# Gate products of three groups summed in two PSUM banks, and the order of the products and output tiles around them

## The chip, the cores and the metric

The kernel runs on one core of a Trainium2 chip. The metric is device time in microseconds (us); lower is better. The engines are named as the profile names them: PE (matmuls; PEld is its weight load), DVE (vector), ACT (scalar), POOL (general purpose), SP (which here only issues DMAs). PSUM is the memory that the PE writes: eight banks of 512 fp32 columns in each of 128 partitions.

## The reference

One layer of an encoder on 512 frames of width 1024. Three branches (gated linear attention, forgetting attention, attention into 256 memory tokens) are merged by sigmoid gates; an output projection and a squared-ReLU MLP follow. What the change touches is the merge:

```python
u = rmsnorm(h, g_mix[l])
proj = u @ w_in[l]                       # its last 3 x 1024 columns are the gates
y_gla = o_gla.reshape(B, S, GLA_V) @ w_gla_o[l]
y_mem = o_mem.reshape(B, S, MEM_W) @ w_mem_o[l]
gt = jax.nn.sigmoid(gates.reshape(B, S, N_BRANCH, D))
merged = gt[:, :, 0] * y_gla + gt[:, :, 1] * y_fox + gt[:, :, 2] * y_mem
h = h + merged @ w_out[l]
```

## The kernel before

Every fp32 operand is split into a high part (fp32r) and the remainder, and a matmul becomes three: high by high, high by low, low by high (`mm3`, lines 154 to 157). Weights come as raw tiles by DMA; `split_w` casts them on ACT to the high part (L145) and subtracts on DVE for the low part (L146).

The gates of the memory branch and of the gated-linear branch are computed in four groups, two for each branch (groups 0 to 3 here; `gate_group`, called at L1043 to L1050). A group makes four gate tiles of 128 channels by 512 frames, as two by two blocks, and does it by a Strassen-Winograd scheme: seven block products (numbered 1 to 7) in place of eight, on sums of weight blocks and sums of input blocks. The sums of inputs (S1 to S4, `lefts_1`, `lefts_2`) are made once, in group 0. The sums of weights are made by DMA: `plus` lets POOL issue a DMA that adds a block of weights in DRAM onto a tile in SBUF (L923). `total` and `other` are these two tiles; in turn `total` is the operand of products 1, 5, 6 and 4, and `other` of product 7. A sum can be issued only when the split that reads the tile before is done.

A product is 24 matmuls of 256 columns into one PSUM bank from a pool of four (`product`, L937), two halves `a` of 256 columns, each its own accumulation group. `take` (L946) then brings it out: the seven results are added in SBUF tiles `ct` by DVE (L932) after ACT copies of products 1 and 5 (L948, L953), and ACT takes tanh of the finished blocks (L935). Here c11, c12, c21 and c22 are the four blocks; c11 and c21 lie in one `ct` tile, c12 and c22 in the other.

Between the products stand the branch's own output tiles: `output(j)` is 12 matmuls of 512 columns into a bank of another pool of four (`a` in the profile); a group has four of them. `merge(j)` (L977) multiplies the gate into the output tile on DVE (L979), and POOL adds it to the accumulator `acc` (L980). In groups 2 and 3 ACT and DVE then split the accumulator for the output projection (L983, L984: `mh`, `ml`), which follows group 3 (L1089): it walks over four weight tiles and for each over four frame tiles, whose PSUM tiles come from the same pool as the output tiles.

The order on the PE is the order of the program. On the other engines a scheduler orders by its own model of time; `issue_after` adds constraints. Each engine runs its own list in order, so an instruction that waits holds up what is behind it. For groups 1 to 3 (`ready is None`) the order on the PE is: product 1, product 2, output j+2, product 5, output j+3, product 3, product 6, product 7, output j, product 4, output j+1. Group 0 starts while the stage before still runs and has an order of its own.

Of the kernel before, what the change touches and what calls it, by code (L numbers as in the profile page):

```python
# [13 lines left out]
AF = mybir.ActivationFunctionType  # L14
ALU = mybir.AluOpType
AX = mybir.AxisListType

P = 128
# [46 lines left out]
def hybrid_block(ctx, tc, chunks, wst, memT, xN, cols, gffn, gfin, wup, cst, out):  # L65
    nc = tc.nc
# [5 lines left out]
    def nm(s):  # L72
        uid[0] += 1
        return f"{s}_{uid[0]}"
# [10 lines left out]
    def mmt(shape=None):  # L85
        return pmm.tile(shape or [P, 512], F32, tag="mm", name=nm("mm"))

    def at_(shape=None):
        return pa.tile(shape or [P, 512], F32, tag="a", name=nm("a"))

    def f(ap):
        return ap.bitcast(F32)
# [27 lines left out]
    chunk_n, cast_now, low_now = [0], [None], [None]  # L120
# [21 lines left out]
    def split_w(raw):  # L142
        hi = wp.tile([P, 1024], F32R, tag="hi", name=nm("whi"))
        lo = wp.tile([P, 1024], F32R, tag="lo", name=nm("wlo"))
        cast = nc.scalar.copy(hi, raw)  # L145
        low_now[0] = nc.vector.tensor_tensor(lo, raw, f(hi), op=ALU.subtract).ins  # L146
        cast_now[0] = cast.ins
        next_sum(cast.ins)
        return hi, lo
# [4 lines left out]
    def mm3(ps, lh, ll, rh, rl, start, stop, on=False):  # L154
        nc.tensor.matmul(ps, lh, rh, start=start, stop=False, skip_group_check=on)  # L155
        nc.tensor.matmul(ps, lh, rl, start=False, stop=False, skip_group_check=on)  # L156
        nc.tensor.matmul(ps, ll, rh, start=False, stop=stop, skip_group_check=on)  # L157
# [29 lines left out]
    def run(*gens):  # L187
        for g in gens:
            for _ in g:
                pass  # L190
# [60 lines left out]
    with pool("front") as fp:  # L251
# [25 lines left out]
        ps = at_()  # L277
# [449 lines left out]
    with pool("gla") as lp:  # L727
# [115 lines left out]
        ready = []  # L843
# [4 lines left out]
        xsum = {}  # L848
# [13 lines left out]
    def h_tile(t, name):  # L862
        return hp.tile([P, D], F32, tag=f"h{t}", name=nm(name))
# [18 lines left out]
    with pool("outp") as op_:  # L882
        def own_tile(i, g):
            return op_.tile([P, 1024], F32R, tag=f"f{i}{g}", name=nm(f"f{i}{g}"))
# [4 lines left out]
        S1, S2, S4 = ([quad(own_tile(i, g)) for g in "hl"] for i in range(3))  # L889
# [9 lines left out]
                split(*S3, xsum[3])  # L899

        def lefts_2(to, block):
            with tc.issue_after(low_now[0]):
                nc.vector.tensor_tensor(xsum[1], block[0], xsum[1], op=ALU.subtract)
                nc.vector.tensor_tensor(xsum[1], xsum[1], block[1], op=ALU.add)
                cast = nc.scalar.copy(to[0], xsum[1]).ins
                nc.vector.tensor_tensor(to[1], xsum[1], f(to[0]), op=ALU.subtract)
            return cast
# [3 lines left out]
        def gate_group(gate, wo, oh, ol, i, ready=None, last=None):  # L911
            src = {b: wst[index["W", gate, i, b]] for b in ("11", "12", "21", "22")}
            total, other = (h_tile(2 * (i % 2) + n, "wb") for n in range(2))
            X = [op_.tile([P, 2, S], F32, tag=f"ct{n}", name=nm("ct")) for n in range(2)]
            (c11, c21), (c12, c22) = ([x[:, :, 256 * n:256 * n + 256] for n in range(2)] for x in X)
            nc.sync.dma_start(total, src["11"])
            first = nc.sync.dma_start(other, src["12"]).ins

            before = summed[0]

            def plus(to, b):
                with tc.issue_after(before) if before is not None else ExitStack():
                    summed[0] = nc.gpsimd.dma_start(to, src[b], accum_op=ALU.add).ins  # L923

            def block(b):
                raw = wp.tile([P, 1024], F32, tag="raw", name=nm("raw"))
                with tc.issue_after(first):
                    loaded[0] = nc.sync.dma_start(raw, src[b]).ins
                return raw

            def vec(to, x, y, op=ALU.add):
                nc.vector.tensor_tensor(to, x, y, op=op)  # L932

            def tanh(x):
                nc.scalar.activation(x, x, AF.Tanh, scale=0.5)  # L935

            def product(n, w):  # L937
                wh, wl = (t.rearrange("p (a k c) -> p a k c", a=2, k=4) for t in w)
                uh, ul = GATE[n]
                ps = mmt([P, 2, 256])  # L940
                for a in range(2):
                    for k in range(4):
                        mm3(ps[:, a, :], wh[:, a, k, :], wl[:, a, k, :], uh[:, k, :], ul[:, k, :], k == 0, k == 3)
                return ps

            def take(n, ps):  # L946
                if n == 1:
                    nc.scalar.copy(c21, ps)  # L948
                if n == 2:
                    vec(c11, c21, ps)  # L950
                    tanh(c11)
                if n == 5:
                    nc.scalar.copy(c22, ps)  # L953
                if n == 6:
                    vec(c21, c21, ps, ALU.subtract)
                    vec(c22, c22, c21, ALU.subtract)
                if n == 3:
                    vec(c12, c22, ps)
                    tanh(c12)
                if n == 7:  # L960
                    vec(c22, c22, ps, ALU.subtract)
                    tanh(c22)
                    vec(c21, c21, ps)
                if n == 4:
                    vec(c21, c21, ps)
                    tanh(c21)

            ys = {}

            def output(j):  # L970
                if j % 2 == 0:
                    with tc.issue_after(first):
                        ys["w"] = get_o(wo, j)
                ys[j] = at_()
                run(o_tile(ys["w"], j, oh, ol, ys[j]))

            def merge(j):  # L977
                th = X[j % 4 // 2][:, j % 2, :]
                nc.vector.scalar_tensor_tensor(th, th, 1.0, ys[j], op0=ALU.add, op1=ALU.mult)  # L979
                nc.gpsimd.tensor_tensor(acc[j], acc[j], th, op=ALU.add)  # L980
                if last is not None:
                    h, l = last
                    nc.scalar.mul(h[:, j, :], acc[j], 0.5)  # L983
                    nc.vector.scalar_tensor_tensor(l[:, j, :], acc[j], 0.5, f(h[:, j, :]), op0=ALU.mult, op1=ALU.subtract)  # L984

            j = 4 * i
            if ready is None:
                take(1, product(1, split_w(total)))
            if ready is not None:
                with tc.issue_after(first):  # L990
                    ys["w"] = get_o(wo, j + 2)
                p1 = product(1, ready[0])
                with tc.issue_after(low_now[0]), tc.issue_after(cast_now[0]):
                    lefts_1()
                    vec(total, total, other)
                    take(1, p1)
            else:
                plus(total, "12")
            plus(other, "22")
            take(2, product(2, ready[1] if ready else split_w(block("21"))))  # L1000
            if ready is None:
                output(j + 2)
            else:
                for n in (2, 3):
                    ys[j + n] = at_()
                    run(o_tile(ys["w"], j + n, oh, ol, ys[j + n]))
            w = split_w(total)
            cast = cast_now[0]
            p5 = product(5, w)
            plus(total, "22")  # L1010
            if ready is not None:
                cast = lefts_2(S2, A11)
                with tc.issue_after(cast):
                    take(5, p5)
                p7 = product(7, split_w(other))
            else:
                take(5, p5)
                output(j + 3)
                p3 = product(3, split_w(block("22")))
            with tc.issue_after(cast):  # L1020
                w = split_w(total)
            take(6, product(6, w))
            plus(total, "21")
            if ready is not None:
                cast = lefts_2(S4, A12)
                output(j)
                p3 = product(3, split_w(block("22")))
            take(3, p3)
            if ready is None:
                p7 = product(7, split_w(other))  # L1030
            take(7, p7)
            merge(j + 2)
            merge(j + 3)
            if ready is None:
                output(j)
            with tc.issue_after(cast):
                w = split_w(total)
            take(4, product(4, w))
            merge(j)
            output(j + 1)  # L1040
            merge(j + 1)

        gate_group("gate_mem", "w_mem_o", omh, oml, 0, ready=ready)  # L1043
        gate_group("gate_mem", "w_mem_o", omh, oml, 1)
# [446 lines left out]
```

## Time and profile before

| | us |
|---|---|
| median of 3 runs (lowest, highest) | 826.78 (825.54, 827.36) |
| the profiled execution's own time | 825.34 |
| its span in the profile | 823.5 |
| PE busy | 812.9 (99%) |
| DVE busy | 602.8 (73%) |
| ACT busy | 457.7 (56%) |
| POOL busy | 104.8 (13%) |

Times in the rows of the profile are microseconds from the span's start. A row of a timeline has the start, the duration, the engine, the line, the operation, the tile written and the tiles read, the shapes and a count; in brackets stands the idle time of the engine ahead of it and what ended it. Rows of one kind that follow each other are merged ("x2"). Instructions of one engine may overlap by some 0.1 us, since an engine is pipelined.

### The profile page before, as it was taken

To read this page: it belongs to the slowest core of one execution; us is meant where nothing else is said; L and a number is where in the kernel's file an instruction comes from. 1 tells how busy PE (TensorE), PEld (TensorE's weight loads), DVE (VectorE), ACT (ScalarE), POOL (GpSimd) and SP (SyncE) were. 2 spreads that over 40 slices of the span, in tenths; PEclk is the share of its full clock that TensorE was granted. 3 is DMA by queue.
4 is the path that set the end of the run, shared out by engine and by line. 5 is a ranking of instruction groups with operands and counts; after the bars stand their busy time and mean duration, and the time that the engine had idled before them with its cause. 6 is when DMAs were issued, how large, how long until landed. Compare 5 with 4: busy or idle time off the path is not lost.

```text
span 823.5 us, 12442 instructions
## 1 busy us (share of the span) xinstructions
PE 812.9 (99%) x4759; PEld 715.6 (87%) x4759; DVE 602.8 (73%) x946; ACT 457.7 (56%) x717; POOL 104.8 (13%) x129
## 2 busy tenths in 40 slices
PE   8999999999999999999999999999999999999996
PEld 6788888888888888999999889988998899889984
DVE  5846887766555686886586647897689778887896
ACT  7765776653345233544344436775577367647764
POOL 1001100101102020132231100011001100110011
PEclk9999999999999999999999999999999999999999
DMA  9534666789687885677665513979758865896654
GB/s 334 182 102 159 189 191 195 195 215 289 156 253 232 228 234 149 131 191 191 153 198 161 186 44 127 274 164 208 244 187 170 220 224 174 187 245 200 161 82 128
DMA packets 39180, 155.60 MB, mean 189 GB/s; under 512 B 4880, under 2 KB 5840, under 8 KB 37072
## 3 DMA queue, kind: packets, MB, share of 16 engines
q1 hardware_dynamic: 27712, 95.54, 33.4%
q0 software_dynamic: 9328, 54.01, 31.9%
q10 hardware_dynamic: 2080, 5.26, 1.9%
q8 instruction: 37, 0.61, 0.3%
q14 instruction: 23, 0.19, 0.1%
HBM read 152.65 MB, written 31.49 MB: 224 GB/s over the span
## 4 chain that ended last, share of the span: by engine, by line
PE 94%; DVE 2%; DMA 1%; issue 1%; ACT 1%; POOL 0%; ACTq 0%; POOLq 0%; DVEq 0%
PE mm L155 23%; PE mm L156 23%; PE mm L157 23%; PE a L156 5%; PE a L155 5%; PE a L157 5%; PE a L797 1%; DMA xn<-in_xN_dram 1%; PE a L526 1%; DMA memr<-in_memT_dram 1%; PE a L559 1%; PE a L527 1%; PE a L558 1%; DVE h L1151 1%; DVE lo L1157 0%
## 5 line engine op out<-in xcount | busy, mean ns | idle before, releaser
L155 PE MATMUL mm<-uhi,whi 128*128 128x512 f32 (+1 forms) x352 | 126.1, 358 | 0.0
L157 PE MATMUL mm<-uhi,wlo 128*128 128x512 f32 (+1 forms) x352 | 123.8, 352 | 0.0
L156 PE MATMUL mm<-ulo,whi 128*128 128x512 f32 (+1 forms) x352 | 123.6, 351 | 0.0
L146 DVE TENSOR_TENSOR wlo<-raw,whi 128x1024 fp32r<-128x1024 f32 x68 | 88.1, 1299 | 43.3 <-ACT whi L145 43.0
L145 ACT CAST whi<-raw 128x1024 fp32r<-128x1024 f32 x68 | 71.4, 1050 | 78.6 <-PE mm L156 44.9
L1155 ACT CAST hi<-raw 128x1024 fp32r<-128x1024 f32 x65 | 68.2, 1049 | 49.6 <-PE mm L156 32.7
L1157 DVE TENSOR_TENSOR lo<-raw,hi 128x1024 fp32r<-128x1024 f32 x65 | 79.4, 1222 | 17.7 <-ACT hi L1155 17.7
L157 PEld LDWEIGHTS mm<-uhi,wlo 128*128 128x128 f32 x352 | 66.6, 189 | 9.1
L155 PEld LDWEIGHTS mm<-uhi,whi 128*128 128x128 f32 x352 | 66.7, 189 | 8.3 <-issue 0.3
L156 PEld LDWEIGHTS mm<-ulo,whi 128*128 128x128 f32 x352 | 66.7, 190 | 8.1
L1155 ACT CAST hi<-b 128x1024 fp32r<-128x1024 f32 x40 | 41.9, 1049 | 42.0 <-PE mm L157 25.5
L157 PE MATMUL mm<-u2h,lo 128*128 128x256 f32 x224 | 63.4, 283 | 0.0
L156 PE MATMUL mm<-u2l,hi 128*128 128x256 f32 x224 | 63.4, 283 | 0.0
L155 PE MATMUL mm<-u2h,hi 128*128 128x256 f32 x224 | 63.4, 283 | 0.0
L1341 POOL DMA_DIRECT2D b<-in_wst_dram x32 | 27.3, 854 | 271.3 <-DVE lo L1157 206.7
L1157 DVE TENSOR_TENSOR lo<-b,hi 128x1024 fp32r<-128x1024 f32 x40 | 48.8, 1221 | 14.1 <-ACT hi L1155 14.0
L155 PE MATMUL mm<-hi,ch 128*128 128x512 f32 x136 | 52.9, 389 | 0.0
L156 PE MATMUL mm<-lo,ch 128*128 128x512 f32 x136 | 52.9, 389 | 0.0
L157 PE MATMUL mm<-hi,cl 128*128 128x512 f32 x136 | 52.9, 389 | 0.0
L156 PE MATMUL mm<-u2sl,hi 128*128 128x256 f32 x168 | 47.6, 283 | 0.0
L155 PE MATMUL mm<-u2sh,hi 128*128 128x256 f32 x168 | 47.6, 283 | 0.0
L157 PE MATMUL mm<-u2sh,lo 128*128 128x256 f32 x168 | 47.6, 283 | 0.0
(405 smaller groups left out, 2161.3 us busy)
## 6 DMA issues: line engine op xcount, KB each, us to landing
raw<-in_wst_dram SPq DMA_DIRECT2D x114, 512.0 KB
b<-in_wst_dram POOLq DMA_DIRECT2D x32, 512.0 KB, 5.5
raw<-T SPq DMA_DIRECT2D x28, 512.0 KB
T<-in_wst_dram POOLq DMA_DIRECT2D x12, 1024.0 KB, 9.6
b<-in_wst_dram SPq DMA_DIRECT2D x16, 512.0 KB
wb<-in_wst_dram POOLq DMA_DIRECT2D x15, 512.0 KB, 5.4
wb<-in_wst_dram SPq DMA_DIRECT2D x8, 512.0 KB
T<-in_wst_dram POOLq DMA_DIRECT2D x6, 512.0 KB, 5.3
```

What stands on the lines that cost most here:

```text
L145: cast = nc.scalar.copy(hi, raw)
L146: low_now[0] = nc.vector.tensor_tensor(lo, raw, f(hi), op=ALU.subtract).ins
L155: nc.tensor.matmul(ps, lh, rh, start=start, stop=False, skip_group_check=on)
L156: nc.tensor.matmul(ps, lh, rl, start=False, stop=False, skip_group_check=on)
L157: nc.tensor.matmul(ps, ll, rh, start=False, stop=stop, skip_group_check=on)
L526: nc.tensor.matmul(ps[:, :w], q, K[e][:, 0, :w], start=True, stop=False)
L527: nc.tensor.matmul(ps[:, :w], q, K[e][:, 1, :w], start=False, stop=True)
L558: nc.tensor.matmul(po[:, q0:], vv, PTh[:, c0:c0 + w], start=n == 0, stop=False)
L559: nc.tensor.matmul(po[:, q0:], vv, PTl[:, c0:c0 + w], start=False, stop=n == 3)
L1155: nc.scalar.copy(hi, raw)
L1157: nc.vector.tensor_tensor(lo, raw, f(hi), op=ALU.subtract)
L1341: nc.gpsimd.dma_start(to[i], wst[index["B", q, i, x]], accum_op=ALU.add)
```

## The change

Group 0 keeps its order (the function is now `first_order`), with one sign turned: `lefts_2` now makes S2 as S1 minus A11 in place of A11 minus S1, so that product 6 comes out negated and its `take` adds where it subtracted; S4 is the same as before.

Groups 1 to 3 get a function of their own, `chain_order`. Products 3, 6, 7 and 4 no longer get a bank each: product 3 is summed by the PE onto product 5's bank, and 6, 7 and 4 onto product 1's bank, one after the other. In between, the state of the bank is brought out as it then stands. Two halves share such a bank, so only the first matmul of half 0 starts the group. In place of seven DVE additions, two ACT copies and four tanh a group has three DVE additions, three copies and four tanh, the last of which reads the bank. The order on the PE becomes: product 1, product 2, output j+2, product 5, output j+3, product 3, product 6, output j, product 7, output j+1, product 4. The last two merges of a group (j and j+1) come after product 4.

```diff
         def lefts_2(to, block):
+            op = ALU.subtract if to is S2 else ALU.add
             with tc.issue_after(low_now[0]):
-                nc.vector.tensor_tensor(xsum[1], block[0], xsum[1], op=ALU.subtract)
-                nc.vector.tensor_tensor(xsum[1], xsum[1], block[1], op=ALU.add)
+                nc.vector.tensor_tensor(xsum[1], xsum[1], block[0], op=op)
+                nc.vector.tensor_tensor(xsum[1], xsum[1], block[1], op=op)
...
-            def product(n, w):
+            def product(n, w, on=None, chain=False):
                 wh, wl = (t.rearrange("p (a k c) -> p a k c", a=2, k=4) for t in w)
                 uh, ul = GATE[n]
-                ps = mmt([P, 2, 256])
+                ps = on if on is not None else mmt([P, 2, 256])
                 for a in range(2):
                     for k in range(4):
-                        mm3(ps[:, a, :], wh[:, a, k, :], wl[:, a, k, :], uh[:, k, :], ul[:, k, :], k == 0, k == 3)
+                        mm3(ps[:, a, :], wh[:, a, k, :], wl[:, a, k, :], uh[:, k, :], ul[:, k, :], k == 0 and on is None and not (chain and a), k == 3,
+                            chain or on is not None)
                 return ps
...
                 if n == 6:
-                    vec(c21, c21, ps, ALU.subtract)
+                    vec(c21, c21, ps)
...
+            def chain_order(j):
+
+                p1 = product(1, split_w(total), chain=True)
+                nc.scalar.copy(c11, p1)
+                plus(total, "12")
+                plus(other, "22")
+                p2 = product(2, split_w(block("21")))
+                vec(c11, c11, p2)
+                tanh(c11)
+                output(j + 2)
+                w = split_w(total)
+                cast = cast_now[0]
+                p5 = product(5, w, chain=True)
+                nc.scalar.copy(c22, p5)
+                plus(total, "22")
+                output(j + 3)
+                product(3, split_w(block("22")), p5)
+                nc.scalar.copy(c12, p5)
+                with tc.issue_after(cast):
+                    w = split_w(total)
+                product(6, w, p1)
+                vec(c12, c12, p1, ALU.subtract)
+                tanh(c12)
+                plus(total, "21")
+                output(j)
+                product(7, split_w(other), p1)
+                vec(c22, c22, p1, ALU.subtract)
+                tanh(c22)
+                merge(j + 2)
+                merge(j + 3)
+                output(j + 1)
+                with tc.issue_after(cast):
+                    w = split_w(total)
+                product(4, w, p1)
+                nc.scalar.activation(c21, p1, AF.Tanh, scale=0.5)
+                merge(j)
+                merge(j + 1)
+
+            (first_order if ready is not None else chain_order)(4 * i)
```

More of the change, by code (lines that the diff above doesn't have):

```diff
@@ L984, in merge, with first_order @@
                     nc.vector.scalar_tensor_tensor(l[:, j, :], acc[j], 0.5, f(h[:, j, :]), op0=ALU.mult, op1=ALU.subtract)
[L986 to L989, printed above, removed]
+            def first_order(j):
                 with tc.issue_after(first):
@@ L996, in gate_group @@
                     take(1, p1)
[L997 to L1003, printed above, removed]
+                plus(other, "22")
+                take(2, product(2, ready[1]))
                 for n in (2, 3):
@@ L1006, in gate_group @@
                     run(o_tile(ys["w"], j + n, oh, ol, ys[j + n]))
[L1007 to L1011, printed above, removed]
+                p5 = product(5, split_w(total))
+                plus(total, "22")
                 cast = lefts_2(S2, A11)
@@ L1015, in gate_group @@
                 p7 = product(7, split_w(other))
[L1016 to L1024, printed above, removed]
+                with tc.issue_after(cast):
+                    w = split_w(total)
+                take(6, product(6, w))
+                plus(total, "21")
@@ L1025, in gate_group @@
                 cast = lefts_2(S4, A12)
                 output(j)
[L1027 to L1034, printed above, removed]
-                output(j)
[L1036 to L1040, printed above, removed]
@@ L1041, in gate_group @@
-            merge(j + 1)
+                take(3, product(3, split_w(block("22"))))
+                take(7, p7)
+                merge(j + 2)
+                merge(j + 3)
+                with tc.issue_after(cast):
+                    w = split_w(total)
+                take(4, product(4, w))
+                merge(j)
[5 more added lines that the diff above has]
+                plus(total, "12")
+                plus(other, "22")
+                p2 = product(2, split_w(block("21")))
[6 more added lines that the diff above has]
+                nc.scalar.copy(c22, p5)
+                plus(total, "22")
+                output(j + 3)
+                product(3, split_w(block("22")), p5)
+                nc.scalar.copy(c12, p5)
+                with tc.issue_after(cast):
+                    w = split_w(total)
+                product(6, w, p1)
+                vec(c12, c12, p1, ALU.subtract)
+                tanh(c12)
+                plus(total, "21")
+                output(j)
+                product(7, split_w(other), p1)
+                vec(c22, c22, p1, ALU.subtract)
+                tanh(c22)
+                merge(j + 2)
+                merge(j + 3)
+                output(j + 1)
+                with tc.issue_after(cast):
+                    w = split_w(total)
+                product(4, w, p1)
+                nc.scalar.activation(c21, p1, AF.Tanh, scale=0.5)
+                merge(j)
+                merge(j + 1)
```

## The prediction

> **What bounds the kernel now.** I read the page first (busy shares, slices, chain), then busy time by stage for the three gate groups that the change rewrites, then the timelines of PE, ACT, DVE and POOL in those stages.
>
> ```profile
> span 823.5 us, 12442 instructions
> ...
> PE 812.9 (99%) x4759; PEld 715.6 (87%) x4759; DVE 602.8 (73%) x946; ACT 457.7 (56%) x717; POOL 104.8 (13%) x129
> ...
> PE 94%; DVE 2%; DMA 1%; issue 1%; ACT 1%; POOL 0%; ACTq 0%; POOLq 0%; DVEq 0%
> ```
>
> ```profile
> core 0: us, PE busy (x) PEld busy (x) DVE busy (x) ACT busy (x) POOL busy (x), PEclk, DMA share, GB/s
> 359.20:390.30 31.10, 31.10 (x217) 29.14 (x216) 22.04 (x21) 13.39 (x16) 10.99 (x10) 1.00 0.73 180
> 390.30:421.40 31.10, 31.10 (x217) 29.14 (x217) 19.87 (x22) 13.61 (x17) 9.59 (x8) 1.00 0.75 191
> 421.40:452.50 31.10, 31.10 (x218) 29.14 (x217) 21.92 (x26) 14.86 (x20) 8.14 (x6) 1.00 0.54 153
> ```
>
> The three stretches are groups 1, 2 and 3. In each the PE is busy for the whole 31.10 us at full granted clock, while DVE and ACT have a third to a half of it free. So work taken from DVE or ACT is worth nothing here by itself, and the change cannot shorten these stages unless it takes matmuls away. It can only open gaps in a PE that has none.
>
> **The change, part by part.**
>
> *PE work.* Each group keeps 7 products of 24 matmuls and 4 output tiles of 12; only the order changes (output j ahead of product 7, output j+1 ahead of product 4) and the bank that receives them. Cost 0. A matmul that adds to a bank is no new kind: of a product's 24, 22 add already.
>
> *Vector and scalar work.* Per group 4 DVE adds go (7 to 3), one ACT copy is added, and the last tanh reads the bank.
>
> ```profile
> L932 DVE TENSOR_TENSOR ct<-ct,mm x24: 675/684/689, 334.6 to 450.0; 128x512 f32<-128x512 f32 x24
> L953 ACT COPY ct<-mm x4: 577/578/579, 344.5 to 434.9; 128x512 f32<-128x512 f32 x4
> ```
>
> DVE gets 3 x 4 x 0.68 = 8.2 us back and ACT pays 3 x 0.58 = 1.7 us. Both lie under the busy PE: 0. Group 0 keeps its order; there two subtractions only swap operands: 0. Sign and group flags of the accumulation cost no instruction.
>
> *New waits: what counts.* A product that adds to a bank must wait until the last reader of that bank is done. There are three per group: product 3 waits for ACT's copy of bank 5; product 7 for DVE's subtraction of product 6; product 4 for DVE's subtraction of product 7. Each has one output tile on the PE as cover. Behind the waiting instruction stands everything left on the PE, so what a wait costs is added to the end.
>
> ```profile
> 367.73 0.28 PE L155 MATMUL mm<-f0h,whi 128*128 128x256 f32 x1
> ...
> 370.60 0.40 PE L155 MATMUL a<-omh,whi 128*128 128x512 f32 x1
> ```
>
> ```profile
> 373.35 0.28 PE L155 MATMUL mm<-f2h,whi 128*128 128x256 f32 x1
> ...
> 404.47 0.28 PE L155 MATMUL mm<-f2h,whi 128*128 128x256 f32 x1
> ...
> 435.59 0.28 PE L155 MATMUL mm<-f2h,whi 128*128 128x256 f32 x1
> ```
>
> Product 5 of group 1 starts at 367.73, the output tile at 370.60, product 3 at 373.35: a product is 2.87 us, the cover 2.75. The three rows of f2h are the starts of product 3 in groups 1 to 3, 31.12 apart.
>
> ```profile
> L146 DVE TENSOR_TENSOR wlo<-wb,whi x19: 1212/1226/1935, 335.2 to 443.2; 128x1024 fp32r<-128x1024 f32 x19
> ```
>
> For products 7 and 4 the reader is one 0.68 us subtraction. In the built order the only DVE work that can stand ahead of it is the split of the next weights, 1.23 us, 1.94 at most: 0.68 + 1.94 = 2.62 fits under 2.75. Cost 0; without that cover up to 2.6 us each.
>
> Product 3 is different. On ACT, both before and after, the copy of bank 5 stands behind the cast of product 6's weights, and that cast waits for an accumulating DMA from POOL:
>
> ```profile
> 367.03 0.87 POOL L923 DMA_DIRECT2D wb<-in_wst_dram  x1
> ...
> 396.48 0.88 POOL L923 DMA_DIRECT2D wb<-in_wst_dram  x1 [1.38 <-DVE wlo L146]
> ...
> 428.34 0.88 POOL L923 DMA_DIRECT2D wb<-in_wst_dram  x1 [1.98 <-DVE wlo L146]
> ```
>
> ```profile
> 372.51 1.05 ACT L145 CAST whi<-wb 128x1024 fp32r<-128x1024 f32 x1 [3.08 <-DMA wb<-in_wst_dram]
> 373.47 0.58 ACT L953 COPY ct<-mm 128x512 f32<-128x512 f32 x1
> ...
> 402.95 0.58 ACT L953 COPY ct<-mm 128x512 f32<-128x512 f32 x1
> ...
> 433.92 1.05 ACT L145 CAST whi<-wb 128x1024 fp32r<-128x1024 f32 x1 [4.02 <-DMA wb<-in_wst_dram]
> 434.88 0.58 ACT L953 COPY ct<-mm 128x512 f32<-128x512 f32 x1
> ```
>
> From issue to cast 5.48 us (367.03 to 372.51) and 5.58 (428.34 to 433.92); the copy starts 0.96 after the cast. It ends at 374.05, 403.53 and 435.46, against product 3 at 373.35, 404.47 and 435.59. Today nobody waits for it. After the change the PE does, and in group 1 it is 0.70 us late.
>
> What a late operand costs is shown once, in group 0:
>
> ```profile
> 349.46 1.23 DVE L906 TENSOR_TENSOR f2l<-x,f2h 128x1024 fp32r<-128x1024 f32 x1
> ...
> 350.19 0.19 PEld L155 LDWEIGHTS mm<-f2h,whi 128*128 128x128 f32 x1
> 350.41 0.28 PE L155 MATMUL mm<-f2h,whi 128*128 128x256 f32 x1
> ...
> 350.74 0.19 PEld L156 LDWEIGHTS mm<-f2l,whi 128*128 128x128 f32 x1 [0.37 <-DVE f2l L906]
> ...
> 350.97 0.28 PE L157 MATMUL mm<-f2h,wlo 128*128 128x256 f32 x1
> ```
>
> The wait holds the weight load, which runs 0.22 ahead of its matmul (350.19, 350.41); it restarts 0.05 after the operand (350.69, 350.74). At the product's pace of 0.12 it was due at 350.31, so it was 0.43 late; the matmul at 350.97 was due at 350.65, so 0.32 was lost. Loss = lateness less 0.11.
>
> [...]
>
> *Group 1.* Nothing ahead of this copy is changed. Load due at 373.35 - 0.22 = 373.13, released at 374.10: 0.97 late, **0.86 lost** (0.7 to 1.0).
>
> *Groups 2 and 3.* Here the copy itself moves, because product 4 now ends the group: its tanh, the two merges and POOL's two adds come one output tile later, and POOL issues the DMA after those adds.
>
> ```profile
> 387.73 1.05 ACT L145 CAST whi<-raw 128x1024 fp32r<-128x1024 f32 x1 [2.72 <-PE mm L156]
> 388.68 0.63 ACT L935 ACTIVATE ct<-ct 128x512 f32<-128x512 f32 x1
> ...
> 390.82 1.27 DVE L979 SCALAR_TENSOR_TENSOR ct<-ct,a 128x512 f32<-128x512 f32 x2
> ...
> 391.57 3.53 POOL L980 TENSOR_TENSOR acc<-acc,ct 128x512 f32<-128x512 f32 x2 [1.77 <-DVE ct L979]
> ...
> 422.50 3.85 POOL L980 TENSOR_TENSOR acc<-acc,ct 128x512 f32<-128x512 f32 x2 [2.68 <-DVE ct L979]
> ```
>
> Group 2, all 0.86 later: product 4 of group 1 ends where product 1 of group 2 starts, 404.47 - 3 x 2.87 - 2 x 2.75 + 0.86 = 391.2; cast 391.3, with its split on DVE until 393.7 ahead of the merges; adds from 394.4 for 3.5 (row 391.57), to 397.9; DMA and cast 5.4, so 403.3; copy until 404.9. Load due at 404.47 + 0.86 - 0.22 = 405.1: in time, **0** (0 to 0.3). Group 3: product 4 ends at 422.3, merges from 424.8, adds 425.5 for 3.85 (row 422.50) to 429.3, DMA to 434.8, copy until 436.4; load due at 436.2: 0.2 late, **0.1 lost** (0 to 0.8; the upper end if the adds take 0.7 longer).
>
> *The end of group 3.* Output j+1 covered product 4's tanh and merge; now the output projection follows at once, and its third tile takes the bank that merge j frees.
>
> ```profile
> 452.56 1.06 ACT L145 CAST whi<-raw 128x1024 fp32r<-128x1024 f32 x1 [0.30 <-PE a L156]
> ...
> 453.67 0.67 DVE L979 SCALAR_TENSOR_TENSOR ct<-ct,a 128x512 f32<-128x512 f32 x1
> ```
>
> ```profile
> 452.59 0.39 PE L155 MATMUL a<-whi,mh 128*128 128x512 f32 x1
> ...
> 455.31 0.39 PE L155 MATMUL a<-whi,mh 128*128 128x512 f32 x1
> ```
>
> Product 4 ends at 452.59 + 0.95 = 453.5. ACT then casts (from 453.6) ahead of the tanh; on DVE that cast's split, until 455.9, stands ahead of merge j (0.67), which ends at 456.6. The third tile's load is due at 455.31 + 0.95 - 0.22 = 456.0: 0.6 late, **0.45 lost** (0.2 to 0.7). The later rows of the projection need acc j only 10.9 us after its start (48 matmuls at 0.227): 0. SP keeps its loads far ahead: 0.
>
> Sum: 0.86 + 0 + 0.1 + 0.45 = 1.4 us on the profiled execution's 825.34, whose span is 823.5: 826.7. The median of the three runs, 826.78, is 1.44 above that execution, so **828.2**.
>
> **The rivals.**
>
> *Not slower.* One mechanism: the copy of bank 5 meets its cover in group 1. It decides at 373.13; the copy must end 0.97 earlier, so POOL's DMA at 367.03 must. For it: groups 2 and 3 of the profile have 0.94 and 0.13 to spare. Against: group 1's queues ahead of it are unchanged. With merge j in time too: 826.8.
>
> *All margins fail.* The later adds push the DMA in both groups and merge j is late: 0.3 + 0.8 + 0.7 on top of 0.86 is 2.7, so 829.5. For it: one row has the adds at 3.85, and DVE and POOL rows stretch when they overlap. Against: 0.2 us in hand in group 2.
>
> *The clock falls.* If the product after each of four gaps ran at half the pace, 4 x 2.87 = 11.5, so 838. For it: the gaps are new. Against: PEclk is 1.00 in all three stages, with DVE, ACT and DMA as busy as they will be. [...]
>
> *Faster.* Freed DVE time would have to shorten a PE wait; the three stages show none. 825.0 at best, by scatter.
>
> **How the numbers follow.** Three small gaps 0.62; not slower 0.12; all margins fail 0.18; clock 0.03; faster 0.05. The median can tell about 0.2% (1.65 us) from no change. The likeliest case, 827.5 to 828.9, lies across that bound: 0.30 of its 0.62 is slower, 0.31 same, 0.01 faster. Slower: 0.30 + 0.18 + 0.03 = 0.51. Same: 0.31 + 0.11 = 0.42. Faster: 0.07. The range reaches from the not-slower case less scatter (826.3) to the failed margins plus scatter (830.0).
>
> **What would show it.** In the profile after: a PE gap of about 0.9 us ahead of product 3 in group 1, released by ACT's copy from mm; none or under 0.3 us there in group 2; up to 0.8 in group 3; none ahead of products 7 and 4; one of about 0.45 at the projection's third tile, released by DVE's merge; DVE busy down by some 8 us, PE unchanged. I am wrong if the copy runs ahead of the cast of product 6, if gaps stand ahead of products 7 or 4, or if PEclk falls.

## The result, and the profile after

| us | before | after |
|---|---|---|
| median of 6 runs (lowest, highest) | 825.89 (825.22, 827.36) | 829.56 (828.83, 830.06) |
| the profiled execution's own time | 825.34 | 830.06 |
| its span | 823.5 | 828.3 |

The ratio after to before is 1.0042 (95% interval 1.0033 to 1.0052): slower by 3.7 us, where 828.2 was predicted. A later series of the same two kernels, told below, gave 828.19 against 825.65, 2.5 us. Which chip ran the first series is not on record; the experiments name theirs.

From the page of the kernel after, the busy shares and the chain of work that ended last:

```profile
PE 814.1 (98%) x4759; PEld 715.1 (86%) x4759; DVE 600.3 (72%) x934; ACT 459.0 (55%) x720; POOL 104.1 (13%) x129
...
PE 44%; DVE 2%; issue 1%; ACT 0%; POOL 0%; POOLq 0%; DVEq 0%; ACTq 0%
```

The PE's share of the chain was 94% before. Now the chain covers only 47% of the span (44, 2 and 1): followed back from the end, it breaks off 47% of 828.3 before it, at 439, beside a wait that the kernel before did not have. The waits of the PE in the stretch from 359 to 470 (what waited, for whom; us in total, times, longest) name it:

```profile
PE mm L155 <- ACT ct L1037: 1.9, 2, 1.4
PE a L155 <- DVE ct L981: 0.5, 1, 0.5
```

L1037 is ACT's copy of bank 5, L981 DVE's merge. Busy time by stage, over the stretches that were shown of before and with the same columns:

```profile
359.20:390.30 31.10, 30.54 (x206) 27.96 (x205) 19.18 (x18) 12.73 (x16) 9.58 (x10) 1.00 0.68 169
390.30:421.40 31.10, 31.10 (x218) 29.03 (x217) 18.01 (x17) 13.16 (x17) 9.48 (x10) 1.00 0.72 186
421.40:452.50 31.10, 29.75 (x209) 27.64 (x208) 20.00 (x19) 14.65 (x20) 7.58 (x7) 1.00 0.60 153
```

The PE is short of its 31.10 us in the first and third stretch, and full in the second. The granted clock stays at 1.00, so the loss is in gaps. The timeline of PE at those places:

```profile
369.13 0.28 PE L155 MATMUL mm<-f0h,whi 128*128 128x256 f32 x1
...
372.00 0.40 PE L155 MATMUL a<-omh,whi 128*128 128x512 f32 x1
...
375.47 0.38 PE L155 MATMUL mm<-f2h,whi 128*128 128x256 f32 x1 [0.56 <-ACT ct L1037]
375.69 0.28 PE L156 MATMUL mm<-f2l,whi 128*128 128x256 f32 x1
...
406.69 0.30 PE L155 MATMUL mm<-f2h,whi 128*128 128x256 f32 x1
...
435.08 0.40 PE L155 MATMUL a<-og,whi 128*128 128x512 f32 x1
...
439.34 0.39 PE L155 MATMUL mm<-f2h,whi 128*128 128x256 f32 x1 [1.35 <-ACT ct L1037]
...
457.83 0.39 PE L155 MATMUL a<-whi,mh 128*128 128x512 f32 x1
...
459.87 0.50 PE L155 MATMUL a<-whi,mh 128*128 128x512 f32 x1 [0.52 <-DVE ct L981]
```

- Product 5 of group 1 starts at 369.13 against 367.73 before: 1.40 us were lost ahead of the changed code, in stages that it does not touch. In the later series the same kernel starts it at 367.81, so this is scatter of single executions, and the span's difference of 4.8 holds it.
- Group 1: product 3 was due one output tile (2.75) after 372.00, at 374.75, and starts at 375.47: 0.72, and 0.10 more because the next matmul follows after 0.22 in place of 0.12. **0.82 lost.**
- Group 2: product 3 at 406.69, 406.70 by the output tile's start at 403.95. **Nothing lost.**
- Group 3: due at 435.08 + 2.75 = 437.83, started at 439.34, and 0.1 as in group 1. **1.6 lost.**
- The output projection: the third tile was due 6 x 0.23 after the second, at 459.2, and starts at 459.87; its first matmul takes 0.50 in place of 0.39. **0.8 lost.**

Together 3.2 us; with the 1.4 that is 4.6 of the 4.7 between the profiled executions. Between the medians lie 3.7; where the other 0.5 goes, one profile does not show.

### The profile page after: what moved, and what is told of

The parts are those of the page before. It is cut to its first block, busy times and chain, and to the rows that moved or that the text cites. A ratio compares the mean times of both kernels' runs of the same rounds, so it can differ in the third digit from the quotient of the medians.

```text
span 828.3 us, 12432 instructions
## 1 busy us (share of the span) xinstructions
PE 814.1 (98%) x4759; PEld 715.1 (86%) x4759; DVE 600.3 (72%) x934; ACT 459.0 (55%) x720; POOL 104.1 (13%) x129
## 5 line engine op out<-in xcount | busy, mean ns | idle before, releaser
L146 DVE TENSOR_TENSOR wlo<-raw,whi 128x1024 fp32r<-128x1024 f32 x68 | 90.4, 1334 | 39.6 <-ACT whi L145 39.3
```

## The experiments

**Theory:** the PE waits at product 3 for ACT's copy of bank 5 (groups 1 and 3) and at the projection's third tile for merge j. **Rival 1:** summing onto a bank in use is itself slow. **Rival 2:** the new order costs it all, and the waits only sit where time would be lost anyway. The first four kernels ran on one chip; the kernel before took 825.54 us there (27 runs). The changed kernel itself was measured on that chip later and is 2.5 over, so that is what the first two of them stand against, and not 3.7.

**The copy ahead of the cast.**

```diff
-                nc.scalar.copy(c22, p5)
+                copied = nc.scalar.copy(c22, p5).ins
...
-                with tc.issue_after(cast):
+                with tc.issue_after(cast), tc.issue_after(copied):
                     w = split_w(total)
                 product(6, w, p1)
```

> The changed kernel with one thing moved: on ACT the copy of bank 5 stands ahead of the cast of product 6's weights instead of behind it; all sums in the banks stay. Theory (the PE waits at product 3 for that copy, 0.83 us in group 1 and 1.6 us in group 3, and 0.8 us at the end of group 3 for merge j): both waits ahead of product 3 vanish, the end's 0.8 stays, so about 0.8 us over the kernel before (ratio 1.001) instead of 3.7. Rival 1 (summing onto a bank that is in use is itself slower, whoever reads it): about 3.7 us over the kernel before, as the changed kernel. Rival 2 (the new order of output tiles and merges costs it all, product 3 would be late anyway): also about 3.7, with a gap of 0.7 to 1.7 us left ahead of product 3, ended by something else.

Measured: 826.59 us, ratio 1.0013 (1.0005 to 1.0022), 1.05 over the kernel before. The waits of its PE in the stretch from 359 to 470, and ACT in group 3:

```profile
PE a L155 <- DVE ct L981: 0.5, 1, 0.5
```

```profile
433.34 0.57 ACT L1037 COPY ct<-mm 128x512 f32<-128x512 f32 x1
435.54 1.05 ACT L145 CAST whi<-wb 128x1024 fp32r<-128x1024 f32 x1 [1.63 <-DMA wb<-in_wst_dram]
```

The copy now starts 2.2 us ahead of the cast, and the wait for it is gone from the list; the one at the end of group 3 stays. All four sums are still made in the banks, so rival 1 falls; the order is still the new one, so rival 2 falls for these two waits.

**Product 3 in a bank of its own.**

```diff
...
-                product(3, split_w(block("22")), p5)
-                nc.scalar.copy(c12, p5)
+                product(3, split_w(block("22")), bank=p2)
+                vec(c12, c22, p2)
```

> The changed kernel with product 3 in another bank (that of product 2, which is free by then), started anew and added by one DVE addition; products 6, 7 and 4 still sum onto bank 1, and the copy of bank 5 stays behind the cast. Theory: nobody waits for the copy, about 0.8 us over the kernel before. Rival 1: three of the four summed products are left, so about three quarters of 3.7, 2.8 us over. Rival 2: 3.7 us over.

Measured: 826.60 us, ratio 1.0012 (1.0003 to 1.0020), 1.06 over. The same time by the other way: with nobody waiting for the copy, it may stay late. The only wait of the PE left in that stretch is again the 0.5 for merge j, so the sums of products 6, 7 and 4, which are still made, add no wait.

**The new order alone, on the kernel before.**

```diff
             if ready is None:
+                output(j)
                 p7 = product(7, split_w(other))
             take(7, p7)
             merge(j + 2)
             merge(j + 3)
             if ready is None:
-                output(j)
+                output(j + 1)
...
             merge(j)
-            output(j + 1)
+            if ready is not None:
+                output(j + 1)
             merge(j + 1)
```

> The kernel before with the new order alone in groups 1 to 3: output j ahead of product 7, output j+1 ahead of product 4, the merges of j and j+1 behind product 4; every product keeps a bank of its own and the DVE additions stay. Theory: only the end of group 3 loses, 0.8 us over the kernel before, with the gap ahead of the third tile of the output projection; none ahead of product 3. Rival 1: no loss (0 within 0.3). Rival 2: about 3.7 us over.

Measured: 829.67 us (5 runs), ratio 1.0040 (1.0026 to 1.0053), 4.1 over. The expectation of 0.8 was wrong, and no gap stands ahead of product 3. Its profile has three other losses. PE and DVE at the end of group 3, and busy time in the 3.4 us that hold the gap and the 3.4 us behind them:

```profile
457.41 0.39 PE L157 MATMUL a<-whi,ml 128*128 128x512 f32 x1
459.70 0.50 PE L155 MATMUL a<-whi,mh 128*128 128x512 f32 x1 [1.91 <-DVE ct L979]
```

```profile
456.64 0.68 DVE L932 TENSOR_TENSOR ct<-ct,mm 128x512 f32<-128x512 f32 x1
457.24 1.22 DVE L146 TENSOR_TENSOR wlo<-raw,whi 128x1024 fp32r<-128x1024 f32 x1
...
458.97 1.27 DVE L979 SCALAR_TENSOR_TENSOR ct<-ct,a 128x512 f32<-128x512 f32 x2
```

```profile
456.66:460.08 3.42, 1.51 (x8) 0.93 (x7) 3.42 (x6) 1.85 (x3) 0.28 (x1) 1.00 0.47 161
460.08:463.49 3.41, 3.41 (x10) 2.65 (x9) 3.41 (x3) 1.83 (x3) 3.23 (x2) 0.50 0.39 125
```

With banks of their own, product 4's result still passes through a DVE addition (456.64) before its tanh and merge. The third tile comes 459.70 - 457.41 = 2.3 us behind the matmul ahead of it, 2.06 more than the usual 0.23. Then the granted clock stands at 0.50 for 3.41 us, in which matmuls start up to 0.43 apart in place of 0.23: nine steps, from 460.04 to 463.69, take 1.6 us more. Another 0.6 goes at product 5 of group 3, whose low weights DVE had not yet split. These are the losses of the profiled execution, at 831.46 us the slowest of the five (the fastest took 827.96); in how many of the others the clock fell is not known. So order and sums cannot be priced apart and added: the sum of product 4 in bank 1, which lets tanh read the bank directly, saves at the end of group 3 most of what the order costs there.

**Product 3's sum alone, on the kernel before.**

```diff
-            p5 = product(5, w)
+            p5 = product(5, w, chain=ready is None)
...
-                p3 = product(3, split_w(block("22")))
+                p3 = product(3, split_w(block("22")), p5)
...
-                    vec(c12, c22, ps)
+                    vec(c12, ps, c21, ALU.subtract)
```

> The kernel before with one sum alone: product 3 onto bank 5, the old order kept, the other three products in banks of their own. Theory: group 1 loses 0.85 us at product 3 as in the changed kernel, group 2 nothing, group 3 0 to 0.2 because POOL's additions of the merges come as early as in the kernel before: 0.85 to 1.05 us over it. If group 3 loses 1.6 here too, the later merges are not what makes it late (2.4 over). Rival 2: 0.

Measured: 826.63 us, ratio 1.0011 (1.0002 to 1.0020), 1.09 over. Its profile, of the median execution, loses 0.5 at product 3 of group 1, where 0.85 was expected, and nothing in groups 2 and 3; the rest of the 1.09 it does not place. ACT and POOL in group 3, with product 3 starting at 436.87 by the PE's timeline:

```profile
435.79 0.58 ACT L954 COPY ct<-mm 128x512 f32<-128x512 f32 x1
```

```profile
429.62 0.88 POOL L923 DMA_DIRECT2D wb<-in_wst_dram  x1 [1.98 <-DVE wlo L146]
```

```profile
436.87 0.28 PE L155 MATMUL mm<-f2h,whi 128*128 128x256 f32 x1
```

The copy ends at 436.37, in time. The DMA is issued 7.3 us ahead of product 3's start; in the changed kernel it is 432.19 against a due 437.83, 5.6 us. So group 3's loss in the changed kernel (1.6 us, and 1.3 on this chip) needs both parts of the change, the sum that makes the PE wait and the order that makes the copy late.

**Both waits removed.** This kernel, the one with short additions, the order-only kernel with the fix and the one with three copies ran on another chip, where the kernel before took 825.92 us (23 runs).

```diff
     def split_w(raw, behind=None):
...
-        low_now[0] = nc.vector.tensor_tensor(lo, raw, f(hi), op=ALU.subtract).ins
+        with tc.issue_after(behind) if behind is not None else ExitStack():
+            low_now[0] = nc.vector.tensor_tensor(lo, raw, f(hi), op=ALU.subtract).ins
...
+        def late_w(key):
+            return split_w(load_w(key), merged[0] if key[2] == 4 else None)
...
-        run(gN([("N", "w_out", 2 * j, 0) for j in range(4)], of(mh, ml), NT, at_, res_evac(0)))
+        run(gN([("N", "w_out", 2 * j, 0) for j in range(4)], of(mh, ml), NT, at_, res_evac(0), get=late_w))
```

To this (`merged[0]` is the last merge) comes the edit of the first experiment.

> The changed kernel with two things moved: the copy of bank 5 ahead of the cast on ACT, and, at the end of group 3, the split of the output projection's third weights on DVE behind the merges of j and j+1 instead of ahead of them. Theory: no wait of the change is left, 0 to 0.3 us over the kernel before (ratio 1.0000 to 1.0004), 0.8 under the run with the first edit alone. Rival: the third tile of the projection is late for tanh or for the merge itself, not for the split ahead of it on DVE: then 0.8 to 1.1 over as with the first edit alone.

Measured: 825.83 us, ratio 0.9997 (0.9988 to 1.0005). The stretch of the three groups:

```profile
359.00:452.00 93.00, 93.00 (x645) 87.06 (x644) 59.01 (x53) 42.35 (x53) 27.30 (x24) 1.00 0.67 175
```

The PE is busy for 93.00 of 93.00 us, as before the change. No wait of the change is left, and what remains of it is the time of the kernel before, with a DVE busy for 600.3 us in place of 602.8.

**The end's fix alone, and the changed kernel again.** The split behind the merges, without the copy's edit, ran beside the changed kernel and the one with two copies in a later series, on the chip of the first four kernels (kernel before 825.65 us, 20 runs).

> The changed kernel itself once more, beside the kernel before on the same chip, to see how its three losses repeat: 3.3 to 3.8 us over the kernel before; product 3 loses 0.7 to 0.9 in group 1, under 0.2 in group 2 and 1.3 to 1.7 in group 3, the projection's third tile 0.7 to 0.9. Rival (the three losses depend on how PE and the DMAs fall against each other in an execution): a loss outside these bounds, with a total that follows.

> The changed kernel with the second of the two fixes alone: on DVE the split of the projection's third weights behind the merges of j and j+1; the copy of bank 5 stays behind the cast. Theory: the end's 0.8 goes and the two waits at product 3 stay, 2.5 to 2.9 us over the kernel before, the gaps of the two places being independent. Rival (the end is late because group 3 is late): the end's 0.8 stays, 3.3 to 3.8 over.

Measured: the changed kernel 828.19 us, ratio 1.0030 (1.0020 to 1.0040), 2.5 over; with the fix 827.59, ratio 1.0021 (1.0012 to 1.0029), 1.9 over. Both totals are under what was expected, because the waits at product 3 are smaller in this series. The changed kernel's PE here:

```profile
367.81 0.28 PE L155 MATMUL mm<-f0h,whi 128*128 128x256 f32 x1
...
373.86 0.39 PE L155 MATMUL mm<-f2h,whi 128*128 128x256 f32 x1 [0.27 <-ACT ct L1037]
...
433.44 0.40 PE L155 MATMUL a<-og,whi 128*128 128x512 f32 x1
437.38 0.39 PE L155 MATMUL mm<-f2h,whi 128*128 128x256 f32 x1 [1.03 <-ACT ct L1037]
...
457.91 0.50 PE L155 MATMUL a<-whi,mh 128*128 128x512 f32 x1 [0.52 <-DVE ct L981]
```

Group 1 loses 373.86 - (367.81 + 5.62) + 0.1 = 0.5, group 3 loses 437.38 - 436.19 + 0.1 = 1.3, the end 0.8 again: 2.6, against 2.5 between the medians (5.62 is a product and an output tile, 436.19 is 433.44 + 2.75). With the fix the gap at the third tile is gone and the two others stay (0.6 and 1.3): the end is independent of what group 3 loses. The rival that the losses depend on how PE and DMAs fall against each other holds for product 3, by 0.3 us a group. The 0.3 us are the transfer's: from POOL's issue to the cast of product 6's weights it took 5.46 us in group 1 and 5.57 in group 3 in the first series (368.43 to 373.89, 432.19 to 437.76), and 5.14 and 5.24 here (367.13 to 372.27, 430.55 to 435.79). Two more profiles of this chip have 5.08 (the copy ahead of the cast, 367.24 to 372.32) and 5.16 (product 3's sum alone, 367.80 to 372.96) in group 1.

**POOL's additions cut short.** Here 504 of the 512 columns of group 2's share of the merge are left out.

```diff
-                nc.gpsimd.tensor_tensor(acc[j], acc[j], th, op=ALU.add)
+                n = 8 if gate == "gate_gla" and i == 0 else S
+                nc.gpsimd.tensor_tensor(acc[j][:, :n], acc[j][:, :n], th[:, :n], op=ALU.add)
```

> The changed kernel with POOL's four additions of group 2's merges cut to 8 of 512 columns (504 columns of group 2's share of the gate result are left out); instructions, DMAs and waits stay. Theory (in group 3 the DMA is late because the splits on DVE are stretched while POOL adds): the split of product 5's weights in group 3 takes 1.2 us instead of 2.33 and ends some 2 us earlier, POOL issues the DMA about 2 us earlier, and the 1.6 us ahead of product 3 in group 3 go; group 1's 0.83 and the end's 0.8 stay: about 1.6 to 2.1 over the kernel before instead of 3.7. Rival (the later merges alone, in POOL's order, delay the DMA; DVE is not slowed): the split keeps its 2.33 or the DMA its time, 3.7 over.

Measured: 827.94 us, ratio 1.0026 (1.0016 to 1.0036), 2.0 over. Group 3 loses nothing at product 3; 0.8 each are left in group 1 and at the end. Why is seen where the DMA of product 6's weights is issued. First the changed kernel, DVE and POOL:

```profile
421.89 3.44 DVE L146 TENSOR_TENSOR wlo<-raw,whi 128x1024 fp32r<-128x1024 f32 x1 [0.18 <-ACT whi L145]
...
428.18 1.46 DVE L986 SCALAR_TENSOR_TENSOR ml<-acc,mh 128x512 fp32r<-128x512 f32 x1
429.57 2.33 DVE L146 TENSOR_TENSOR wlo<-wb,whi 128x1024 fp32r<-128x1024 f32 x1
```

```profile
421.38 2.85 POOL L982 TENSOR_TENSOR acc<-acc,ct 128x512 f32<-128x512 f32 x2
427.81 3.01 POOL L982 TENSOR_TENSOR acc<-acc,ct 128x512 f32<-128x512 f32 x2 [3.57 <-DVE ct L981]
432.19 0.88 POOL L924 DMA_DIRECT2D wb<-in_wst_dram  x1 [1.38 <-DVE wlo L146]
```

Then the kernel with short additions:

```profile
427.04 1.22 DVE L146 TENSOR_TENSOR wlo<-wb,whi 128x1024 fp32r<-128x1024 f32 x1 [0.42 <-ACT whi L145]
```

```profile
428.57 0.88 POOL L924 DMA_DIRECT2D wb<-in_wst_dram  x1 [1.60 <-DVE wlo L146]
```

In the changed kernel POOL is done at 430.82 and stands idle for 1.38 us: the DMA waits for DVE's split of product 5's weights, and that split took 2.33 us beside POOL's additions, with another of 3.44 in the queue ahead of it. With short additions it takes 1.22 and the DMA goes out 3.6 us earlier; 0.7 of that is the execution's own (the output tile ahead of product 3 starts at 434.37 in place of 435.08), so against the PE it is 2.9 earlier. The scheduler also moved one `ml` ahead and one split back when the additions shrank, so not all of the 2.9 is the stretching; that the split takes longer beside POOL's additions is shown by the durations, 2.33 us against 1.22.

**A longer gap, and the clock.** Three kernels ask whether the clock falls behind a longer gap, as in the order-only kernel. In the first, the split stands behind the merges there too (the edit of both waits removed, without the copy's). In the others ACT copies bank 5 three times, or twice, in the changed kernel.

```diff
-                nc.scalar.copy(c22, p5)
+                for _ in range(3):
+                    nc.scalar.copy(c22, p5)
```

> The order-only kernel with that split on DVE behind the merges. Order alone lost 4.1 us: by its trace 0.6 at product 5 of group 3, 2.1 ahead of the projection's third tile, and 1.8 in the 3.5 us behind that gap, in which the granted clock stood at 0.51. Theory A (the long gap itself takes the clock down): the gap shrinks to about 1.1, the clock stays at 1.00, about 1.3 us over the kernel before. Theory B (the clock falls there for another reason): the gap shrinks but the clock still falls, about 3.1 over.

> The changed kernel with the copy of bank 5 done three times on ACT in each of the groups 1 to 3: product 3 has to wait some 1.0 us longer in each. Theory A: gaps of about 1.9 us in group 1, 1.0 in group 2 and 2.6 in group 3, 3.0 us over the changed kernel (6.7 over the kernel before) from the waits, and 1.8 us more for each gap of 2 us and above, where the clock falls to half for 3.5 us: 8.5 over the kernel before with one, 10.3 with two. Theory B (gaps do not move the clock): 6.7 over, granted clock 1.00 behind all three. If nobody waited for the copy: 3.7 over.

> The changed kernel with the copy of bank 5 done twice: product 3 waits 0.5 us longer, so that about 1.4 are lost in group 1, 0.6 in group 2 and 2.2 in group 3. Theory A' (the length of the gap alone decides over the clock; 1.9 lost left it at 1.00, 2.06 and 2.8 lost took it to half): the clock falls behind group 3's gap and costs 1.6 more, 6.8 us over the kernel before. Theory B' (the length does not decide alone): 2.2 lost, clock still 1.00, 5.2 over.

Measured: order-only with the fix 827.90 us, ratio 1.0027 (1.0017 to 1.0036), 2.0 over; three copies 834.13 (4 runs), 1.0103 (1.0090 to 1.0116), 8.2 over; two copies 829.64 (5 runs), 1.0050 (1.0037 to 1.0062), 4.0 over. The waiting matmuls with three copies, two stretches around each of them, then the one of group 3 with two copies, and the third tile of the order-only kernel with the fix (its lines are one or two later):

```profile
375.42 0.39 PE L155 MATMUL mm<-f2h,whi 128*128 128x256 f32 x1 [1.76 <-ACT ct L1038]
...
441.88 0.39 PE L155 MATMUL mm<-f2h,whi 128*128 128x256 f32 x1 [2.65 <-ACT ct L1038]
```

```profile
371.21:374.63 3.42, 2.45 (x11) 1.69 (x9) 0.95 (x1) 1.99 (x3) 0.00 (x0) 1.00 0.59 195
374.63:378.04 3.41, 2.62 (x21) 2.62 (x22) 1.50 (x2) 1.65 (x3) 1.76 (x2) 1.00 0.41 55
...
439.48:442.89 3.41, 1.01 (x8) 1.01 (x9) 1.30 (x2) 3.24 (x5) 0.86 (x1) 1.00 0.02 10
442.89:446.31 3.42, 3.42 (x18) 3.42 (x17) 1.15 (x1) 0.00 (x0) 0.00 (x0) 0.50 0.95 162
```

```profile
438.88 0.39 PE L155 MATMUL mm<-f2h,whi 128*128 128x256 f32 x1 [1.66 <-ACT ct L1038]
```

```profile
456.74 0.50 PE L156 MATMUL a<-whi,mh 128*128 128x512 f32 x1 [0.95 <-DVE ct L980]
```

Behind idle times of 1.66 and 1.76 us the clock stayed at 1.00; behind 1.91 (order only) and 2.65 it fell to half. In the order-only kernel with the fix the idle time shrank to 0.95 and the clock stayed, which is theory A; but the profile is of a short execution (826.93 us), the median of 827.90 lies between the two expectations, and what the longer executions lost is not shown. With three copies 8.2 over is near theory A with one such gap (8.5), and the profile has one. With two copies group 3 lost 1.9 and not 2.2, because the changed kernel itself loses only 1.3 there on this chip; that run did not reach the length in question.

The order-only kernel's clock stands at 0.50 for one stretch of 3.41 us. In the kernels before and after, the full clock lasts 812.38 and 819.20 us (7.33 to 819.71 and 6.64 to 825.84), 238 and 240 times 3.413. Counted in stretches of that length, as in the tables above, the 1.76 us fall as 0.97 into one and 0.79 into the next (3.42 - 2.45, 3.41 - 2.62), and the clock stayed at 1.00; the stretch ahead of each fall holds 1.91 us (3.42 - 1.51) and 2.40 (3.41 - 1.01) of idle PE. In the changed kernel the clock stays at 1.00 behind the stretch that holds the 1.35 us of group 3, and falls to 0.50 behind one without a matmul at the program's end:

```profile
436.72:440.13 3.41, 2.06 (x12) 1.52 (x11) 1.22 (x1) 2.37 (x3) 0.00 (x0) 1.00 0.42 161
440.13:443.55 3.42, 3.42 (x31) 3.42 (x30) 1.25 (x2) 1.21 (x3) 0.86 (x1) 1.00 0.49 62
822.43:825.84 3.41, 0.00 (x0) 0.00 (x0) 1.03 (x3) 1.00 (x3) 0.55 (x1) 1.00 0.57 222
825.84:828.30 2.46, 0.00 (x0) 0.00 (x0) 0.00 (x0) 0.00 (x0) 0.00 (x0) 0.50 0.31 118
```

The idle time within a stretch puts these cases in order, and so does the length of the single gap (1.76 us at most without a fall, 1.91 and 2.65 with one). No kernel was made to tell the two apart, and what decides over the clock is not shown.

## Why the prediction was right in sign and range, and where it was short

*Nothing to gain.* Right. With both waits removed the changed kernel takes the time of the kernel before. DVE was to be busy 8.2 us less and is 2.5 less: the additions are gone, but splits such as the two of 3.44 and 2.33 us take part of it back (the 87 splits of L146 take 116.0 us in place of 112.6).

*Products 7 and 4 at no cost.* Right: no wait of theirs in any profile of the changed kernel.

*Group 1, 0.86.* Right: 0.82, and 0.5 in the later series, where the transfer was 0.3 us shorter. The copy that was late is the one named, behind the cast that was named. ACT in the changed kernel (the last three rows are of groups 2 and 3), and the weight load that waited:

```profile
373.89 1.05 ACT L145 CAST whi<-wb 128x1024 fp32r<-128x1024 f32 x1 [3.05 <-DMA wb<-in_wst_dram]
374.84 0.58 ACT L1037 COPY ct<-mm 128x512 f32<-128x512 f32 x1
...
405.98 0.58 ACT L1037 COPY ct<-mm 128x512 f32<-128x512 f32 x1
...
437.76 1.04 ACT L145 CAST whi<-wb 128x1024 fp32r<-128x1024 f32 x1 [2.26 <-PE a L156]
438.71 0.58 ACT L1037 COPY ct<-mm 128x512 f32<-128x512 f32 x1
```

```profile
375.47 0.19 PEld L155 LDWEIGHTS mm<-f2h,whi 128*128 128x128 f32 x1 [0.98 <-ACT ct L1037]
```

The copy ended at 375.42 and the load restarted 0.05 later. By the prediction's rule (load due at 374.75 - 0.22, loss = lateness less 0.11) that is 0.83, and 0.82 was lost. The load itself waited, as in the row at 350.74.

*Group 2, 0.* Right, with nothing to spare: the copy ends at 406.56, the load was due at 403.95 + 2.75 - 0.22 = 406.48 and starts at 406.61. Of these 0.13 us 0.11 cost nothing by the same rule, which leaves 0.02.

*Group 3, 0.1 with a bound of 0.8.* Wrong: 1.6, and 1.3 in the later series. The failed step is "adds 425.5 for 3.85 (row 422.50) to 429.3, DMA to 434.8". It lets the DMA go when POOL's additions end. The row of before that the prediction itself quotes, the DMA at 428.34, says otherwise in its bracket: POOL had been idle for 1.98 us and DVE's split released it. The term is that split, put at nothing, and it is late twice over: it stands behind the later merges, and it is stretched beside their additions. The rest of the step held. The additions end at 430.82, 6.8 us ahead of the load's due time of 437.83 - 0.22, where the prediction has 6.9 (429.3 to 436.2), and from issue to cast it takes 5.57 us (432.19 to 437.76) against 5.58. What is left is POOL's idle 1.38 us: 0.1 and 1.4 are 1.5 of the 1.6 measured. (The bracket of the cast at 437.76 names a matmul; the profile has the transfer landing 5.5 us after its issue, at 437.7, and in the later series the same cast is put down to the DMA.)

*The end, 0.45 (0.2 to 0.7).* Right place and releaser, too small: 0.8 in both profiles. The chain of ACT's cast, DVE's split and merge j is the one predicted; what was left out is a DVE instruction ahead of the split that took 1.78 us beside POOL's additions (454.01 to 457.54), where the same instruction took 0.68 at 433.56 with POOL idle:

```profile
456.30 1.78 DVE L986 SCALAR_TENSOR_TENSOR ml<-acc,mh 128x512 fp32r<-128x512 f32 x1
458.00 1.21 DVE L146 TENSOR_TENSOR wlo<-raw,whi 128x1024 fp32r<-128x1024 f32 x1
459.14 1.27 DVE L981 SCALAR_TENSOR_TENSOR ct<-ct,a 128x512 f32<-128x512 f32 x2
```

*The sum.* 1.4 was predicted; the profiles lose 3.2 and 2.6, the medians differ by 3.7 and 2.5. "All margins fail" (2.7) came closest, though not as it was told: group 2 held and group 3 lost twice its upper bound. The range held because it reached to that rival, which for group 3 is luck: its upper end stood for later additions, and not for the split. The likeliest case was too small by the term of group 3 and by half the end's.

*The clock* did not fall behind the changed kernel's three waits, the longest of them 1.35 us of idle time. The 0.03 for a fall was the author's estimate: the kernel before has no gaps in these stages that could show what one does to the clock. In the order-only kernel it fell to 0.50 behind 1.91 us, so gaps not much longer were not safe.

## What to carry to other kernels

When an engine that is 100% busy is made to wait for a reader it did not need before, the price is set by the whole queue ahead of that reader: here a copy of 0.58 us behind a cast of 1.04, behind a DMA that takes 5.57 from issue to cast, behind a split of 2.33 on another engine (group 3). Follow each release to the row that names it, also where the idle time in its bracket cost nothing so far; and free the reader first (a copy ahead of the cast), since then the same sums cost nothing: 825.83 us with both waits removed, 825.92 before. Two parts of one edit may need or mend each other, so a part tried alone is not its share of the whole.

## What was not expected of the hardware

In these rows DVE instructions with two inputs in SBUF took longer beside POOL's additions. The split that takes 1.22 us alone took 3.44 (421.89, beside additions from 421.38 to 424.23) and 2.33 (429.57, beside additions until 430.82) in the changed kernel. In the kernel before, one took 1.72 (423.48) and an `ml` 1.78 (425.12, 0.68 at 427.96) beside additions from 422.50 to 426.35; another `ml` (422.27), beside the first 0.46 us of them, kept 0.69. The merges, with one input in PSUM, kept their time: 0.68 at 422.88 in the kernel before, beside the same additions, as at 421.68 ahead of them, and 0.68 on average over all 16 in both kernels. What the two engines contend for, no run shows.

PE idle times of 1.91 and 2.65 us were followed by a half-speed clock (0.50) for 3.41 us, at a cost of about 1.5 to 1.6 us each (16 matmuls 0.21 apart in place of 0.12 in the second case), while behind 1.66 and 1.76 it stayed at 1.00.
